# Moving five small tiles ahead of the stationary operands in SBUF

## The chip, the core and the metric

One core of a Trainium2 chip runs the whole kernel as one program. The metric is the device time of one execution in microseconds (us); of several executions the median is given. The engines are TensorE (PE in the profile, its weight loads PEld), VectorE (DVE), ScalarE (ACT), GpSimd (POOL) and SyncE (SP, which issues most transfers).

## The reference

One layer of a decoder trunk on x of 256 x 2048 in float32:

```python
h = h + 0.5 * swiglu_ffn(rms_norm(h, ffn1_norm), ffn1_w_gate, ffn1_w_up, ffn1_w_down)   # 2048 -> 5632 -> 2048
hn = rms_norm(h, mix_norm)
proj = hn @ w_in                                     # q | k | v | u, 1024 columns each
attn = mixture_of_dilations(rms_norm(q), rms_norm(k), v, rel_bias)   # 8 heads of 128
y = s5_ssm(u, lambda, log_dt, b, c, d)               # 64 groups of 16 channels, 64 complex states each
y = gelu(y); y = y * sigmoid(y @ glu_w + glu_b)
h = h + concat([attn, y]) @ w_out
h = h + 0.5 * swiglu_ffn(rms_norm(h, ffn2_norm), ffn2_w_gate, ffn2_w_up, ffn2_w_down)

def swiglu_ffn(x, w_gate, w_up, w_down):
    return (silu(x @ w_gate) * (x @ w_up)) @ w_down
```

## The kernel before, in words

The big products are all done by one loop, `run` (lines 247 to 330), over a list of passes: 22 gate and up passes and 4 down passes of the first feed-forward (`ffn`), the mixer's passes (`w_in`, `glu_w`, `w_out`), then 22 and 4 again. A pass makes 512 output columns for all 256 rows. Its weights come in groups of four blocks of 128 rows, 1 MB each, into `raw` (three buffers, SyncE's queue). Each group is handled as two units. For a unit, ScalarE writes the high part of the weights, rounded to the matmul's reduced format, to `wh` (line 281), and VectorE the rest, `raw - wh`, to `wl` (line 286); four buffers each let the splits run ahead of TensorE by up to four units. Then TensorE does twelve matmuls of 128 x 128 by 128 x 512: for each of two blocks and two halves of the rows, high by high (line 325), high by low (326) and low by high (327). The weights `wh`, `wl` are the moving operand, 512 columns at a time; the stationary operand is 128 x 128 of the transposed activations, also in a high and a low tile:

- in the gate and up passes and in `w_in`: `xth` and `xtl`, four pairs of tiles [128, 4, 256] in the pool `const` (class `Normed`, `open`, lines 156 and 157);
- in the down passes: `hid`, tiles [128, 2, 4, 256] (high and low together) in the pool `slots`;
- in `glu_w` and `w_out`: tiles in `slots` as well, which the profile calls by their tags `slot`, `s4b`, `s2a` and `s2b`.

A gate and up result is turned for the down product by `by_blocks` (line 124): VectorE transposes it in 32 x 32 blocks into `blocks`, a transfer writes that to memory (`h_d`), four transfers bring it back into `sil`, and ScalarE and VectorE split it into `hid` (lines 119, 120). The code of such side work is in generators, each advanced one step after every unit (`step`), so its instructions stand in each engine's queue between the splits, in a fixed order.

During the first feed-forward `ssm_prepare` computes the tables of the state-space model in this way, most of it VectorE's work (the powers in lines 654 to 656). In the mixer, `ssm_run` does the scan on VectorE (lines 767 to 769), and the attention's heads go on beside it.

SBUF is laid out when the program is built. The pools lie one behind the other, `const`, `slots`, `rawp`, `wp`, `sm`, `sm1`. Within a pool a tile takes its place when its tag is first asked for, right behind the tile before it, its size rounded up to 32 bytes of a partition. `slots` starts at the next place behind the last tile of `const`.

Of the kernel before, what the change touches and what calls it, by code (L numbers as in the profile page):

```python
# [9 lines left out]
F32 = mybir.dt.float32  # L10
# [6 lines left out]
P = 128  # L17
# [29 lines left out]
def hybrid_layer_kernel(  # L47
# [10 lines left out]
    const = ctx.enter_context(tc.tile_pool(name="const", bufs=1))  # L58
# [19 lines left out]
    def small(shape, tag):  # L78
        p = sm1 if tag in ("rel", "knc") else sm
        return p.tile(list(shape), F32, name=nm(tag), tag=tag)  # L80

    def tps():
        return tpp.tile([P, 512], F32, name=nm("tp"), tag="tp")
# [7 lines left out]
    rq = const.tile([P, 2, 8], F32, name="rq", tag="rq")  # L91
    stat = const.tile([P, NH, 8], F32, name="stat", tag="stat")
    a8 = const.tile([P, 2, 2, NG], F32, name="a8", tag="a8")

    m1_d = dram.tile([4, 4, P, 512], F32, name="m1_d", tag="m1_d")
    m2_d = dram.tile([4, P, 2048], F32, name="m2_d", tag="m2_d")
# [121 lines left out]
    def spawn(g, delay=0):  # L218
        gens.append([g, delay])
        return g  # L220
# [177 lines left out]
    def residual(norm, factor):  # L398
        def done(n):
            def f(acc):  # L400
                for t in range(NT):
                    vec.scalar_tensor_tensor(out=res[n][:, t, :], in0=acc[t], scalar=factor,
                                             in1=res[n][:, t, :], op0=ALU.mult, op1=ALU.add)
                spawn(norm.feed(n) if n == 3 else norm.feed_by_blocks(n))
            return f
        return done

    def final(n):
        def f(acc):
            for t in range(NT):  # L410
                vec.scalar_tensor_tensor(out=res[n][:, t, :], in0=acc[t], scalar=0.5,
                                         in1=res[n][:, t, :], op0=ALU.mult, op1=ALU.add)
                (sync if n == 3 else pool).dma_start(out=out[0, t * P:(t + 1) * P, n * 512:(n + 1) * 512], in_=res[n][:, t, :])
        return f


    def ssm_prepare():
# [3 lines left out]
        def T():  # L421
            i = tmpi[0]
            tmpi[0] += 1
            assert i < 36
            return a3[:64, i * 64:(i + 1) * 64]

        lr, li = T(), T()
        ldt = const.tile([64, 1], F32, name="ldt", tag="ldt")
        pool.dma_start(out=ldt, in_=ssm_log_dt[0].rearrange("(g o) -> g o", o=1))
        pool.dma_start(out=lr, in_=ssm_lambda_re[0])  # L430
        pool.dma_start(out=li, in_=ssm_lambda_im[0])
# [36 lines left out]
            vec.scalar_tensor_tensor(out=em, in0=p2, scalar=-1.0, in1=e, op0=ALU.add, op1=ALU.add)  # L468
            res_.extend((ex, em))

        col = const.tile([64, 8], F32, name="dtcol", tag="dtcol")
        ci = [0]

        def newcol():
# [153 lines left out]
        ps = tps()  # L628
        pe.transpose(ps[:, 0:16], dpad.rearrange("q j c -> q (j c)"), ident[:16, :16])
        yield  # L630
        dcol = const.tile([P, 16], F32, name="dcol", tag="dcol")
        act.activation(out=dcol, in_=ps[:, 0:16], func=AF.Copy)
        dmask = const.tile([P, 16], F32, name="dmask", tag="dmask")
        vec.tensor_tensor(out=dmask, in0=ident[:, 0:16], in1=ident[:, 32:48], op=ALU.add)
        vec.tensor_tensor(out=dmask, in0=dmask, in1=ident[:, 64:80], op=ALU.add)
        vec.tensor_tensor(out=dmask, in0=dmask, in1=ident[:, 96:112], op=ALU.add)
# [433 lines left out]
    with tc.manual_schedule():  # L1070
        xin = x[0].rearrange("(t p) d -> p t d", p=P)
        grow = slots.tile([50, P], F32, name="grow", tag="s5a")
        act.dma_start(out=grow[0:16], in_=ffn1_norm[0].rearrange("(k p) -> k p", p=P))
        sync.dma_start(out=res[0][:, :, 0:256], in_=xin[:, :, 0:256])
        warm = const.tile([1, 1], F32, name="warm", tag="warm")
        vec.memset(warm, 0.0)
        act.activation(out=warm, in_=warm, func=AF.Silu)
        make_identity(nc, ident)

        def warm_up(n):  # L1080
            ps = tps()
            for _ in range(n):
                pe.transpose(ps[:, 0:P], ident, ident)

        warm_up(12)
        ps = tps()
        pe.transpose(ps[:, 0:16], grow[0:16], ident[:16, :16])
        vec.tensor_copy(out=gains["f1"], in_=ps[:, 0:16])

        def other_gains():  # L1090
            for i, g in enumerate((mix_norm, ffn2_norm)):
                pool.dma_start(out=grow[16 + 16 * i:32 + 16 * i], in_=g[0].rearrange("(k p) -> k p", p=P))
            pool.dma_start(out=grow[48:49], in_=q_norm)
            pool.dma_start(out=grow[49:50], in_=k_norm)
            pool.memset(flip, 0.0)
            pool.affine_select(out=flip, in_=flip, compare_op=ALU.not_equal, fill=1.0, base=1 - P,
                               pattern=[[1, P]], channel_multiplier=1)
            pool.memset(sgn[0:64], 1.0)
            pool.memset(sgn[64:128], -1.0)
            yield 4  # L1100
            ps = tps()
            pe.transpose(ps[:, 0:50], grow, ident[:50, :50])
            for i, key in enumerate(("mx", "f2")):
                vec.tensor_copy(out=gains[key], in_=ps[:, 16 + 16 * i:32 + 16 * i])
            knc = small([P, 1], "knc")
            vec.tensor_copy(out=knc, in_=ps[:, 49:50])
            vec.scalar_tensor_tensor(out=qkg, in0=ps[:, 48:49], scalar=1.0 / math.sqrt(HD), in1=knc,
                                     op0=ALU.mult, op1=ALU.mult)
            yield
            yield from bias_table()  # L1110

        def bias_table():
            rel = small([34, NH], "rel")
            pool.memset(rel, 1.0)  # L1114
            pool.dma_start(out=rel[0:32], in_=rel_bias)
            oh = slots.tile([34, SPAN], F32, name="oh", tag="s1a")
            pool.dma_start(out=oh, in_=bias_rows)
            yield
            yield
            ps = tps()  # L1120
            pe.matmul(ps[:NH, 0:SPAN], rel, oh, start=True, stop=True)
            bt = slots.tile([NH, SPAN], F32, name="bt", tag="s1b")
            vec.tensor_copy(out=bt, in_=ps[:NH, 0:SPAN])
            pool.dma_start(out=b_d, in_=bt)

        n1, nmix, n2 = Normed("f1"), Normed("mx"), Normed("f2")

        feeds = [n1.feed(n, True) for n in range(4)]

        def feed_input():  # L1130
            for n in range(1, 4):
                for _ in feeds[n]:
                    pass
                yield 2 if n < 3 else 1
            spawn(other_gains())
            mx["pre"] = spawn(ssm_prepare(), 1)
            for n in range(4):
                n1.squares(n)
                n1.count()
                yield  # L1140

        def start():
            next(feeds[0], None)
            if "go" not in mx:
                warm_up(4)
            if "go" in mx:
                spawn(feed_input())
            mx["go"] = True

        ff1 = ffn(n1, ffn1_w_gate[0], ffn1_w_up[0], ffn1_w_down[0], residual(nmix, 0.5), True)  # L1150
        mixp = mixer(nmix, residual(n2, 1.0))
        ff2 = ffn(n2, ffn2_w_gate[0], ffn2_w_up[0], ffn2_w_down[0], lambda n: final(n), False)

        def load_x(n):
            if n == 0:
                sync.dma_start(out=res[0][:, :, 256:512], in_=xin[:, :, 256:512])
            elif n < 4:
                sync.dma_start(out=res[n], in_=xin[:, :, n * 512:(n + 1) * 512])

        run(ff1 + mixp + ff2, load_x, start)  # L1160
# [54 lines left out]
```

## Time and profile before

| | |
|---|---|
| median of 3 runs | 1856.63 us (1852.51 to 1858.55) |
| the profiled execution | 1858.62 us, its span 1856.8 us |
| mean granted TensorE clock | 0.993 |
| transferred | 401.23 MB, mean 216 GB/s |

How to read the rows. The span is the time from the first to the last profiled instruction. A group of instructions shows: line, engine, operation, tiles (out<-in), shapes and count, then the time in which at least one of them was under way, the mean duration of one in ns, and how long the engine was idle just before them and for whom. Matmuls overlap: each lasts longer than the distance from its start to the next one's. A row of stretches shows, for PE, PEld, DVE, ACT and POOL, the busy time and the instructions (x) in the stretch, then the granted clock (PEclk), the share of the transfer engines and GB/s; asked for one tile, it shows the instructions of that tile alone and only the engines that have any. A row of the timeline shows start, duration, engine, line, operation, tiles and, in brackets, the idle time before and who ended it. The chain of waits is followed back from the end, at each step to the work that released it; cut to a stretch, its first row gives shares of that stretch by engine and line.

### The profile page before, as it was taken

To read this page: it belongs to the slowest core of one execution; us is meant where nothing else is said; L and a number is where in the kernel's file an instruction comes from. 1 tells how busy PE (TensorE), PEld (TensorE's weight loads), DVE (VectorE), ACT (ScalarE), POOL (GpSimd) and SP (SyncE) were. 2 spreads that over 40 slices of the span, in tenths; PEclk is the share of its full clock that TensorE was granted. 3 is DMA by queue.
4 is the path that set the end of the run, shared out by engine and by line. 5 is a ranking of instruction groups with operands and counts; after the bars stand their busy time and mean duration, and the time that the engine had idled before them with its cause. 6 is when DMAs were issued, how large, how long until landed. Compare 5 with 4: busy or idle time off the path is not lost.

```text
span 1856.8 us, 21467 instructions
## 1 busy us (share of the span) xinstructions
PE 1825.0 (98%) x8389; PEld 1476.3 (80%) x8389; DVE 1061.3 (57%) x1382; ACT 836.1 (45%) x1071; POOL 42.8 (2%) x91
## 2 busy tenths in 40 slices
PE   8999999999999999989999999999999999999999
PEld 6787777788888888867877888888888888888887
DVE  4778788555554555534795665555555555544443
ACT  5444434344444444435566555444444444443332
POOL 2100000000000000010000001000000000000000
PEclk8999999999999999989999999999999999999999
DMA  8676788866766666598556586667666666666562
GB/s 268 204 207 191 252 268 274 258 204 211 216 218 212 208 225 207 194 256 282 181 190 223 202 243 206 205 208 216 214 204 209 218 207 205 218 211 212 197 214 103
DMA packets 220389, 401.23 MB, mean 216 GB/s; under 512 B 9580, under 2 KB 50133, under 8 KB 219136
## 3 DMA queue, kind: packets, MB, share of 16 engines
q1 hardware_dynamic: 214384, 383.29, 65.3%
q0 software_dynamic: 4080, 13.43, 2.3%
q10 hardware_dynamic: 1824, 3.15, 0.6%
q8 instruction: 65, 1.06, 0.2%
q14 instruction: 36, 0.29, 0.0%
HBM read 370.00 MB, written 32.45 MB: 217 GB/s over the span
## 4 chain that ended last, share of the span: by engine, by line
PE 82%; DVE 8%; DMA 6%; ACT 2%; issue 1%; SPq 1%; ACTq 0%; DVEq 0%
PE acc L325 26%; PE acc L326 26%; PE acc L327 26%; DVE wl L286 3%; DMA h_d<-blocks 2%; DMA sil<-h_d 1%; DMA raw<-in_ffn_w_gate_dram 1%; DVE s4b L654 1%; ACT wh L281 1%; DMA raw<-in_w_in_dram 1%; DVE s1a L767 1%; DMA u_d<-s4a 0%; DVE slot L655 0%; DVE s1a L768 0%; DVE s4a L656 0%
## 5 line engine op out<-in xcount | busy, mean ns | idle before, releaser
L286 DVE TENSOR_TENSOR wl<-raw,wh 128x1024 fp32r<-128x1024 f32 x628 | 765.6, 1225 | 669.6 <-ACT wh L281 669.3
L281 ACT ACTIVATE wh<-raw 128x1024 fp32r<-128x1024 f32 (+1 forms) x636 | 667.2, 1057 | 857.4 <-PE acc L327 796.5
L325 PE MATMUL acc<-wh,xth 128*128 128x512 f32 x1664 | 666.5, 401 | 16.9 <-ACT wh L281 16.9
L326 PE MATMUL acc<-wl,xth 128*128 128x512 f32 x1664 | 662.3, 398 | 3.7 <-DVE wl L286 3.5
L327 PE MATMUL acc<-wh,xtl 128*128 128x512 f32 x1664 | 660.4, 397 | 0.0
L325 PEld LDWEIGHTS acc<-wh,xth 128*128 128x128 f32 x1664 | 314.5, 189 | 95.1 <-ACT wh L281 19.5
L326 PEld LDWEIGHTS acc<-wl,xth 128*128 128x128 f32 x1664 | 314.4, 189 | 82.9 <-DVE wl L286 8.7
L327 PEld LDWEIGHTS acc<-wh,xtl 128*128 128x128 f32 x1664 | 314.4, 189 | 75.3
L326 PE MATMUL acc<-wl,hid 128*128 128x512 f32 x704 | 273.9, 389 | 0.0
L327 PE MATMUL acc<-wh,hid 128*128 128x512 f32 x704 | 273.9, 389 | 0.0
L325 PE MATMUL acc<-wh,hid 128*128 128x512 f32 x704 | 273.9, 389 | 0.0
L326 PEld LDWEIGHTS acc<-wl,hid 128*128 128x128 f32 x704 | 132.1, 188 | 27.6
L327 PEld LDWEIGHTS acc<-wh,hid 128*128 128x128 f32 x704 | 132.1, 188 | 27.5
L325 PEld LDWEIGHTS acc<-wh,hid 128*128 128x128 f32 x704 | 132.1, 188 | 27.4
L120 DVE TENSOR_TENSOR hid<-sil,hid 128x512 fp32r<-128x512 f32 x44 | 28.5, 689 | 67.9 <-ACT hid L119 67.9
L119 ACT ACTIVATE hid<-sil 128x512 fp32r<-128x512 f32 x44 | 25.4, 624 | 87.5 <-DMA sil<-h_d 87.5
L369 DVE SCALAR_TENSOR_TENSOR sil<-acc,rstd,sil 128x512 f32<-128x512 f32 x44 | 30.8, 741 | 0.0
L358 ACT ACTIVATE sil<-acc,rstd 128x512 f32<-128x512 f32 x44 | 27.5, 675 | 3.6 <-POOL rel L1114 3.6
L129 DVE STREAM_TRANSPOSE blocks<-sil 128x512 f32<-128x512 f32 x44 | 28.5, 685 | 0.0
L113 POOL TENSOR_TENSOR rs_t<-rstd 128x2 f32<-128x2 f32 x9 | 3.6, 396 | 665.9 <-DVE rstd L110 665.4
L325 PE MATMUL acc<-wh,slot 128*128 128x512 f32 x48 | 18.9, 393 | 0.0
L327 PE MATMUL acc<-wh,slot 128*128 128x512 f32 x48 | 18.7, 390 | 0.0
(324 smaller groups left out, 793.5 us busy)
## 6 DMA issues: line engine op xcount, KB each, us to landing
raw<-in_ffn_w_up_dram SPq DMA_DIRECT2D x88, 1024.0 KB, 5.8
raw<-in_ffn_w_down_dram SPq DMA_DIRECT2D x88, 1024.0 KB, 5.1
raw<-in_ffn_w_gate_dram SPq DMA_DIRECT2D x87, 1024.0 KB, 5.6
raw<-in_w_in_dram SPq DMA_DIRECT2D x32, 1024.0 KB, 5.6
raw<-in_w_out_dram SPq DMA_DIRECT2D x16, 1024.0 KB, 5.8
h_d<-blocks SPq DMA_DIRECT2D x28, 512.0 KB, 6.9
sil<-h_d SPq DMA_DIRECT2D x88, 128.0 KB, 6.9
m_d<-slot POOLq DMA_DIRECT2D x4, 1024.0 KB, 7.0
```

What stands on the lines that cost most here:

```text
L119: act.activation(out=h, in_=src, func=AF.Copy)
L120: vec.tensor_tensor(out=l, in0=src, in1=h.bitcast(F32), op=ALU.subtract)
L129: vec.transpose(out=b[:, :, t].rearrange("p j (k c) -> p j k c", k=4), in_=src[:, t, :].rearrange("p (k j c) -> p j k c", k=4, j=4))
L281: act.activation(out=h[:, c], in_=src[:, c], func=AF.Copy)
L286: vec.tensor_tensor(out=l, in0=src, in1=h.bitcast(F32), op=ALU.subtract)
L325: pe.matmul(acc[t], sh[:, c], h[:, kk, :], start=first, stop=False)
L326: pe.matmul(acc[t], sh[:, c], l[:, kk, :], start=False, stop=False)
L327: pe.matmul(acc[t], sl[:, c], h[:, kk, :], start=False, stop=last)
L358: act.activation(out=sil[c][:, t, :], in_=acc[t], func=AF.Silu, scale=norm.scale(t))
L369: vec.scalar_tensor_tensor(out=a[:, t, :], in0=acc[t], scalar=norm.scale(t), in1=a[:, t, :], op0=ALU.mult, op1=ALU.mult)
L654: vec.tensor_tensor(out=t_, in0=zb, in1=pr, op=ALU.mult)
L767: vec.tensor_tensor(out=tm, in0=a8, in1=prev.unsqueeze(1).broadcast_to([P, 2, 2, NG]), op=ALU.mult)
```

## The change

Five small tiles of the pool `const` are asked for at the start, behind `a8`, instead of where they are first used. Four belong to `ssm_prepare`: `ldt` and `col` (`dtcol`), which were asked for behind `xth` and `xtl`, and `dcol` and `dmask`, which were asked for behind `blocks`. The fifth, `warm`, was asked for at the start of the work and stays in its neighbourhood.

```diff
     a8 = const.tile([P, 2, 2, NG], F32, name="a8", tag="a8")
+    ldt = const.tile([64, 1], F32, name="ldt", tag="ldt")
+    col = const.tile([64, 8], F32, name="dtcol", tag="dtcol")
+    dcol = const.tile([P, 16], F32, name="dcol", tag="dcol")
+    dmask = const.tile([P, 16], F32, name="dmask", tag="dmask")
+    warm = const.tile([1, 1], F32, name="warm", tag="warm")
...
         lr, li = T(), T()
-        ldt = const.tile([64, 1], F32, name="ldt", tag="ldt")
...
-        col = const.tile([64, 8], F32, name="dtcol", tag="dtcol")
         ci = [0]
...
-        dcol = const.tile([P, 16], F32, name="dcol", tag="dcol")
         act.activation(out=dcol, in_=ps[:, 0:16], func=AF.Copy)
-        dmask = const.tile([P, 16], F32, name="dmask", tag="dmask")
...
-        warm = const.tile([1, 1], F32, name="warm", tag="warm")
         vec.memset(warm, 0.0)
```

The instructions of every engine, their order and their waits are the same in both programs; only the addresses of some tiles differ. In bytes of a partition:

| tiles | address before | modulo 512 | address after | modulo 512 |
|---|---|---|---|---|
| `ldt`, `dtcol` | 68512, 68544 | 416, 448 | 35520, 35552 | 192, 224 |
| `dcol`, `dmask` | 72672, 72736 | 480, 32 | 35584, 35648 | 256, 320 |
| `warm` | 35520 | 192 | 35712 | 384 |
| sums and factors of the norms (`ssp`, `rstd`) | 35552 to 35712 | | 35744 to 35904 | |
| `xth`, `xtl`, four pairs | 35744 + n x 4096 | 416 | 35936 + n x 4096 | 96 |
| `blocks` | 68576 | 480 | 68704 | 96 |
| all of `slots` (`hid` and others) | from 72800 | 96 | the same | 96 |
| `raw` | 171104 + n x 8192 | 96 | the same | 96 |
| `wh`, `wl` | 195680 + n x 4096 | 96 | the same | 96 |
| `ident`, `flip`, `res` | 16512 to 33920 | 128 | the same | 128 |

Within a tile, a matmul's operand starts at a multiple of 512 bytes, so the residue of the tile holds for all its operands.

## The prediction

> **What bounds the kernel now.** I read the page's busy times first, then the groups of instructions by line and form, then the busy time by stretches, then TensorE's timeline where one product follows another, and last the chain of waits stretch by stretch.
>
> ```profile
> PE 1825.0 (98%) x8389; PEld 1476.3 (80%) x8389; DVE 1061.3 (57%) x1382; ACT 836.1 (45%) x1071; POOL 42.8 (2%) x91
> L325 PE MATMUL acc<-wh,xth 128*128 128x512 f32 x1664 | 666.5, 401 | 16.9 <-ACT wh L281 16.9
> L327 PE MATMUL acc<-wh,xtl 128*128 128x512 f32 x1664 | 660.4, 397 | 0.0
> L325 PE MATMUL acc<-wh,hid 128*128 128x512 f32 x704 | 273.9, 389 | 0.0
> ```
>
> TensorE is busy 98% of the span. Three groups of 1664 matmuls (4992) take their stationary operand from `xth`/`xtl`, three of 704 (2112) from `hid`. The shape is the same, the moving operands are the same `wh`/`wl` tiles, yet one lasts 397 to 401 ns and the other 389. Matmuls overlap, so the cost is the distance between starts; a row of a long stretch with nothing but big matmuls gives it.
>
> ```profile
> core 0: us, PE busy (x) PEld busy (x) DVE busy (x) ACT busy (x) POOL busy (x), PEclk, DMA share, GB/s
> 540.00:770.00 230.00, 230.00 (x1016) 190.46 (x1015) 120.56 (x127) 99.81 (x111) 0.00 (x0) 1.00 0.65 211
> 1140.00:1600.00 460.00, 460.00 (x1973) 370.65 (x1972) 236.63 (x223) 196.88 (x208) 0.00 (x0) 1.00 0.68 210
> ```
>
> From 540 to 770 us (`hid`) 1016 matmuls, less two that hang over the edges, make 230/1014 = 226.8 ns each; from 1140 to 1600 us (`xth`) 460/1971 = 233.4 ns. TensorE is never idle in either, and the granted clock is 1.00 in both. The `xth` products pay 6.6 ns more per matmul, 4992 x 6.6 = 32.9 us in all. What differs is the address of the stationary tile: `hid` lies at 96 modulo 512 like `wh` and `wl`, `xth` and `xtl` at 416. The switch from one to the other, in TensorE's timeline:
>
> ```profile
> 536.81 0.39 PE L327 MATMUL acc<-wh,xtl 128*128 128x512 f32 x1
> 537.04 0.39 PE L325 MATMUL acc<-wh,hid 128*128 128x512 f32 x1
> ...
> 538.43 0.39 PE L325 MATMUL acc<-wh,hid 128*128 128x512 f32 x1
> 538.65 0.39 PE L326 MATMUL acc<-wl,hid 128*128 128x512 f32 x1
> ```
>
> The six `hid` starts up to 538.43 still lie 0.23 apart (1.39/6 = 232 ns), from there on 0.22 to 0.23 (226.8 as above). So the fast pace sets in some seven matmuls after a disturbance. The same happens where small transposes interrupt products whose stationary tile is also at 96:
>
> ```profile
> 1044.16 0.60 PE L837 MATMUL tp<-ident,s1a 128*128 128x128 f32 x4
> 1044.52 0.47 PE L325 MATMUL acc<-wh,s4b 128*128 128x512 f32 x1
> 1044.83 0.39 PE L326 MATMUL acc<-wl,s4b 128*128 128x512 f32 x1
> ...
> 1046.21 0.39 PE L326 MATMUL acc<-wl,s4b 128*128 128x512 f32 x1
> ```
>
> Between 1044.83 and 1046.21 stand six starts, 230 ns each: an interruption costs the fast pace for about seven matmuls.
>
> **The change part by part.** It removes and adds no instruction, no wait and no transfer, and the order on every engine stays; five small tiles (192 bytes) move ahead, so `xth` and `xtl` go from 416 to 96 modulo 512 and `blocks` from 480 to 96; `wh`, `wl`, `hid` and the rest stay. `ldt`, `col`, `dcol`, `dmask` and `warm` themselves cost the same at another place: no row shows a dependence of VectorE on it, and the changes are multiples of 32 bytes. `blocks` is written by VectorE and read by a transfer; `hid`'s neighbours at 96 do both already; I cost it at nothing.
>
> What remains is 6.6 ns for each of 4992 matmuls, wherever TensorE sets the end. That is what the chain of waits tells, cut into stretches.
>
> ```profile
> by line: DVE wl L286 20.4%; DMA h_d<-blocks 17.3%; DMA sil<-h_d 10.9%; issue 8.0%; DVE s4b L654 6.8%; DVE slot L655 3.9%; DVE s4a L656 3.5%; DVE s4a L655 3.1%; DMA k_d<-slot 3.0%; SPq L690 3.0%; DVE s4b L669 2.8%; DVE sil L369 2.6%; SPq L13
> by line: DVE wl L286 27.6%; DVE s1a L767 13.7%; DVE s1a L768 11.0%; issue 8.1%; DVE slot L769 8.1%; ACT wh L281 4.3%; ACT tp L844 4.0%; DVE rs_t L115 2.4%; DVE rs_t L113 2.3%; DVE rs_t L114 2.3%; DVE s5a L909 2.3%; DVE s5a L907 2.0%; DVE st
> by line: DMA raw<-in_w_in_dram 34.5%; DMA u_d<-s4a 27.8%; DMA slot<-m_d 20.6%; DVE wl L286 3.9%; PE acc L326 3.8%; ACT wh L281 3.3%; PE acc L327 2.7%; ACT s4a L976 2.2%; PE acc L325 1.3%; issue 0.8%; ACTq L281 0.1%; SPq L702 0.1%; SPq L268
> by line: PE acc L327 33.3%; PE acc L325 33.3%; PE acc L326 33.3%; PE tp L184 0.2%
> ```
>
> The first is 152 to 356 us (VectorE's powers of the state-space model, then the turn of a hidden block through `h_d`), the second 886 to 955 (the scan), the third 800 to 832 (loads behind `u_d`), the last 1084 to 1612 (gate and up of the second feed-forward). In the first three TensorE hardly stands in the chain: what it gains there it waits longer. In the last it is all. The other stretches are TensorE's too. How many matmuls of lines 325 and 326 with `xth` each holds (line 327's come to half as many again):
>
> ```profile
> 22.00:152.00 130.00, 110.00 (x343) 64.31 (x343) 3.31 (x8) 3.12 (x8) 0.98 0.69 213
> 152.00:356.00 204.00, 171.81 (x532) 100.11 (x530) 0.00 (x0) 0.00 (x0) 0.99 0.79 252
> 356.00:537.00 181.00, 162.58 (x518) 97.01 (x516) 0.00 (x0) 0.00 (x0) 1.00 0.71 218
> 776.00:800.00 24.00, 20.56 (x66) 12.22 (x66) 1.75 (x4) 1.68 (x4) 1.00 0.62 186
> 832.00:886.00 54.00, 40.93 (x124) 23.22 (x124) 0.00 (x0) 0.00 (x0) 0.97 0.88 281
> 886.00:955.00 69.00, 54.10 (x169) 30.91 (x168) 0.00 (x0) 0.00 (x0) 1.00 0.57 174
> 955.00:1003.00 48.00, 28.76 (x88) 15.95 (x88) 0.00 (x0) 0.00 (x0) 1.00 0.67 235
> 1084.00:1612.50 528.50, 442.21 (x1407) 264.38 (x1408) 8.19 (x28) 5.97 (x15) 1.00 0.69 211
> ```
>
> The terms, times 6.6 ns: 1084 to 1612, 1407 x 1.5 = 2111 matmuls, 13.9 us. 356 to 537, 777, 5.1. 776 to 800, 99, 0.6. In three stretches small work interrupts:
>
> ```profile
> 22.00:152.00 130.00, 130.00 (x571) 103.58 (x570) 90.14 (x179) 67.97 (x107) 5.87 (x18) 0.98 0.69 213
> 832.00:886.00 54.00, 54.00 (x355) 43.07 (x354) 24.18 (x35) 30.10 (x52) 0.00 (x0) 0.97 0.88 281
> 955.00:1003.00 48.00, 47.93 (x445) 39.51 (x446) 30.55 (x68) 28.52 (x56) 0.54 (x1) 1.00 0.67 235
> ```
>
> From 22 to 152 us 571 less 515 leaves 56 small ones; in groups of four to eight that is 7 to 14 interruptions, 50 to 100 matmuls at the old pace, so 2.7 of 3.4 us. From 832 to 886 (186 big ones, 169 small) I take 0.5 of 1.2, from 955 to 1003 (132 and 313) 0.3 of 0.9. The stretches 152 to 356, 800 to 832 and 886 to 955 stand at zero; were they TensorE's after all, they would give 798 x 6.6 = 5.3, 0.7 and 1.7. Sum: 13.9 + 5.1 + 0.6 + 2.7 + 0.5 + 0.3 = 23.1 us.
>
> One cost comes with it. In 152 to 356 us TensorE runs dry four times, and a longer pause can lower its clock:
>
> ```profile
> 197.58 0.40 PE L327 MATMUL acc<-wh,xtl 128*128 128x512 f32 x1
> 199.20 0.50 PE L325 MATMUL acc<-wh,xth 128*128 128x512 f32 x1 [1.23 <-ACT wh L281]
> ...
> 200.92 0.63 PE L327 MATMUL acc<-wh,xtl 128*128 128x512 f32 x1
> ...
> 203.91 0.47 PE L325 MATMUL acc<-wh,xth 128*128 128x512 f32 x1
> 353.91 0.50 PE L325 MATMUL acc<-wh,xth 128*128 128x512 f32 x1 [1.49 <-ACT wh L281]
> ```
>
> After the pause at 197.58 the matmuls up to 203.9 last 0.63 us instead of 0.40 and start 0.43 apart, some 8 x 0.2 = 1.6 us lost. After the one before 353.91 they did not. Each pause grows by what TensorE gains in its 50 us, some 1.3 us, so the last may now be followed by slow matmuls too, and there TensorE sets the end: 0 to 1.6 us, I take 1. The other three lose it inside a stretch that VectorE and the transfers pace.
>
> Covers. Behind TensorE, ScalarE's and VectorE's splits must stay ahead. The tightest place I found outside the three stretches is a turned block that ScalarE waits for in its queue, with the splits behind it:
>
> ```profile
> 1375.37 1.15 ACT L119 ACTIVATE hid<-sil 128x512 fp32r<-128x512 f32 x2 [4.52 <-DMA sil<-h_d]
> 1378.65 3.50 DVE L286 TENSOR_TENSOR wl<-raw,wh 128x1024 fp32r<-128x1024 f32 x3 [1.33 <-ACT wh L281]
> 1381.02 0.40 PE L326 MATMUL acc<-wl,xth 128*128 128x512 f32 x1
> ```
>
> Three `wl` take 3.50 us from 1378.65; the first is done at about 1379.9, and its matmul starts at 1381.02, 1.1 us later. Between the block's issue and this use TensorE does about six units of twelve matmuls, which at 6.6 ns come 0.5 us sooner: the cover holds by 0.6. If it did not, each such block would cost up to 1 us; of the 22 (eleven to each feed-forward) some 16 lie outside the first stretch.
>
> So 23.1 - 1 = 22.1 us off. The profiled execution took 1858.6 us (span 1856.8), so 1836.5; the median of the three runs shown is 2.0 below it, so 1834.5.
>
> **The rivals.** First, no change: the pace hangs on something else in which `xth` differs, for example that it lies in the lower part of the memory, and 192 bytes don't alter that. For it speaks that no row shows a second residue for the same tile; against it that `xtl` of the last block ends 4 KB below `hid`'s first tile, and that h and l, both row halves and all four blocks of `xth` keep the same pace. It gives 1856.6. The Trainium skill, "TensorE: Matmul & The Clock Gate", section "Step-by-step: what each phase is for", is on this side: it says that TensorE has two independent read ports for the moving operand and for the weights, so that loading the next weights takes no read bandwidth from the running matmul. By that rule where the stationary tile lies could not matter and the sum would be zero; the trace's two paces for one shape don't agree with it, though they don't say that the address is the reason.
>
> Second, the covers fail: the turned blocks come late for a TensorE that runs ahead, in both feed-forwards. At 1 us for each of 16 blocks the gain falls to 6 us: 1850.6. The 4.52 us wait above speaks for it, the 1.1 us margin against it.
>
> Third, slower: the clock. The faster pace would last from 1084 to the end, 770 us, while the longest fast stretch now is 244 (1612 to 1857). Were the clock lowered after some 240 us of it, 510 us would run at a lower clock; the 22.1 us are used up at a granted clock of 510/532 = 0.96, and at 0.90 the time is 1834.5 + 57 = 1891. Against it: 540 to 770 us shows 1.00 at the fast pace throughout.
>
> **How the numbers follow.** The pace goes over to the `xth` products: 0.82. No change: 0.08. Covers fail: 0.05. The clock, or another loss above the gain: 0.05. Within 0.3% (5.6 us) is about what a measurement of this kernel can't tell from no change. Faster: 0.82 plus half of the covers' case and a little, 0.85; same 0.10; slower 0.05. The range goes from the full 32.9 us (1823) to what the two steady stretches leave (19.0) less 1.6 for the clock and some 5 us of late blocks (1844); it leaves out no change.
>
> **What would show it.** Right: `xth` groups at 389 to 393 ns instead of 397 to 401; from some point in the second feed-forward a stretch of 460 us holding about 2030 matmuls instead of 1973; that feed-forward's gate and up 14 us shorter; the stretch of the powers about as long as before, with longer pauses. Wrong: starts still 233 ns apart, or 227 with new waits of TensorE for `wh` or `wl` after each `hid`, or a PEclk below 1.00 late in the span.

## The result and the profile after

The changed kernel takes 1833.46 us (median of 4 runs, 1833.28 to 1834.23) against 1856.84 us of the kernel before beside it: a ratio of 0.9875, 95% interval 0.9863 to 0.9888, 23.4 us less. Its profiled execution took 1833.54 us with a span of 1831.8 us, 25.0 less than the span before. Line numbers of the changed kernel are five higher where the large products stand (330 to 332 for 325 to 327).

First the rows of the page and of the busy time by stretches that answer to those in the prediction:

```profile
PE 1798.0 (98%) x8389; PEld 1476.9 (81%) x8389; DVE 1060.3 (58%) x1382; ACT 834.7 (46%) x1071; POOL 43.4 (2%) x91
L330 PE MATMUL acc<-wh,xth 128*128 128x512 f32 x1664 | 658.7, 396 | 16.5 <-ACT wh L286 16.5
L332 PE MATMUL acc<-wh,xtl 128*128 128x512 f32 x1664 | 652.0, 392 | 0.0
L330 PE MATMUL acc<-wh,hid 128*128 128x512 f32 x704 | 274.0, 389 | 0.0
```

```profile
540.00:765.00 225.00, 225.00 (x994) 186.35 (x993) 116.92 (x123) 97.73 (x109) 0.00 (x0) 1.00 0.64 213
1130.00:1580.00 450.00, 450.00 (x1987) 372.64 (x1986) 238.68 (x226) 197.23 (x208) 0.00 (x0) 1.00 0.70 215
```

The engines' instructions are as many as before and `hid` is untouched: 225/992 = 226.8 ns between starts. The `xth` products now run at the same pace, 450/1985 = 226.7 ns, where it was 233.4. The clock is granted in full in both stretches. The chain of waits, cut to the powers of the state-space model and to gate and up of the second feed-forward:

```profile
by line: DVE wl L291 18.5%; DMA h_d<-blocks 16.3%; DMA sil<-h_d 8.6%; issue 6.9%; DVE s4b L655 6.5%; PE acc L331 4.5%; PE acc L332 4.1%; PE acc L330 4.1%; DVE slot L656 3.7%; DVE s4a L657 3.4%; ACT wh L286 3.0%; DVE s4a L656 3.0%; SPq L140 
by line: PE acc L331 33.3%; PE acc L332 33.3%; PE acc L330 33.3%; PE tp L189 0.2%
```

In the first, VectorE and the transfers still lead; TensorE has 13% of it. The second is TensorE's from end to end, as before.

Where the time came from can be read off the starts of the same matmul in two traces, since the order of TensorE's instructions is the same. The table has the length of each stretch in the two profiled executions, and beside it the means over several kernels of the experiments below: six in which the `xth` products start 232 to 234 ns apart (the kernel before and off32, off96, off128, off160, off224), three in which they start 227 ns apart (the changed kernel, all256, off256). Times in the first column are those of the kernel before, in us.

| stretch | before | after | less | mean of six | mean of three | less | predicted |
|---|---|---|---|---|---|---|---|
| 0 to 22, start | 22.0 | 23.2 | -1.2 | 22.5 | 23.0 | -0.6 | 0 |
| 22 to 152 | 130.0 | 126.4 | 3.6 | 129.5 | 126.4 | 3.1 | 2.7 |
| 152 to 356, powers | 203.5 | 200.7 | 2.8 | 202.0 | 201.3 | 0.8 | 0 |
| 356 to 537 | 181.5 | 178.5 | 3.0 | 182.0 | 177.2 | 4.8 | 5.1 - 1 |
| 537 to 776, `hid` | 239.2 | 239.1 | 0.0 | 239.1 | 239.1 | 0.0 | 0 |
| 776 to 800 | 24.0 | 23.4 | 0.6 | 24.0 | 23.4 | 0.6 | 0.6 |
| 800 to 832 | 30.2 | 29.9 | 0.3 | 30.0 | 30.2 | -0.3 | 0 |
| 832 to 886 | 55.8 | 54.4 | 1.4 | 55.1 | 54.3 | 0.8 | 0.5 |
| 886 to 955, scan | 68.9 | 68.9 | 0.0 | 68.9 | 68.9 | 0.0 | 0 |
| 955 to 1003 | 47.9 | 47.5 | 0.5 | 48.2 | 48.0 | 0.2 | 0.3 |
| 1084 to 1612 | 528.6 | 514.6 | 14.0 | 528.6 | 514.6 | 14.0 | 13.9 |

The stretches left out (1003 to 1084, and from 1612 on) are the same within 0.1 us. The last column sums to 22.1, the means to 23.4, the pair to 25.0.

### The profile page after: what moved, and what is told of

The parts are those of the page before. It is cut to its first block, busy times and chain, and to the rows that moved or that the text cites. A ratio compares the mean times of both kernels' runs of the same rounds, so it can differ in the third digit from the quotient of the medians.

```text
span 1831.8 us, 21467 instructions
## 1 busy us (share of the span) xinstructions
PE 1798.0 (98%) x8389; PEld 1476.9 (81%) x8389; DVE 1060.3 (58%) x1382; ACT 834.7 (46%) x1071; POOL 43.4 (2%) x91
## 4 chain that ended last, share of the span: by engine, by line
PE 84%; DVE 8%; DMA 5%; ACT 1%; issue 1%; SPq 1%; ACTq 0%; DVEq 0%
PE acc L330 27%; PE acc L331 27%; PE acc L332 27%; DVE wl L291 3%; DMA h_d<-blocks 2%; DMA sil<-h_d 1%; DMA raw<-in_ffn_w_gate_dram 1%; DVE s4b L655 1%; ACT wh L286 1%; DMA raw<-in_w_in_dram 1%; DVE s1a L768 1%; DVE s1a L769 0%; DVE slot L656 0%; DVE s4a L657 0%; DVE s4a L656 0%
## 5 line engine op out<-in xcount | busy, mean ns | idle before, releaser
L330 PE MATMUL acc<-wh,xth 128*128 128x512 f32 x1664 | 658.7, 396 | 16.5 <-ACT wh L286 16.5
L331 PE MATMUL acc<-wl,xth 128*128 128x512 f32 x1664 | 653.9, 393 | 3.6 <-DVE wl L291 3.2
L332 PE MATMUL acc<-wh,xtl 128*128 128x512 f32 x1664 | 652.0, 392 | 0.0
L330 PE MATMUL acc<-wh,slot 128*128 128x512 f32 x48 | 18.9, 393 | 0.0
L331 PE MATMUL acc<-wl,slot 128*128 128x512 f32 x48 | 18.7, 389 | 0.0
```

Of the source, the lines that this page charges most:

```text
L330: pe.matmul(acc[t], sh[:, c], h[:, kk, :], start=first, stop=False)
L331: pe.matmul(acc[t], sh[:, c], l[:, kk, :], start=False, stop=False)
L332: pe.matmul(acc[t], sl[:, c], h[:, kk, :], start=False, stop=last)
```

## Experiments

Theory A: TensorE's pace in these products depends on where the stationary tile lies relative to the moving one, by their distance modulo some size. Rival B: it depends on the stationary tile's own residue, 96 being a good one. All kernels are variants of the changed kernel unless said otherwise, with unused bytes put ahead of one group of tiles. Each was run once, except the pair at the end of this section (four runs each); a pace is read inside one trace, over 220 or 430 us, and is good to 0.1 to 0.2 ns, since a matmul more or less changes it by that much.

**Everything moved together, and the moving tiles moved alone.** all256 puts 256 bytes ahead of `xth`, so that all operands go from 96 to 352 modulo 512; wp192 puts 192 bytes ahead of `wh` and `wl` in a pool of their own; the pools `sm` and `sm1` behind them move along, no tile of which takes part in these products.

```diff
+    const.tile([P, 64], F32, name="pad_all", tag="pad_all")      # all256, behind a8
...
+    padp = ctx.enter_context(tc.tile_pool(name="padp", bufs=1))  # wp192, between rawp and wp
+    padp.tile([P, 48], F32, name="pad_w", tag="pad_w")
```

> The changed kernel with 256 unused bytes ahead of xth in the pool const: every operand of the big products (xth, xtl, hid, wh, wl) moves from 96 to 352 modulo 512, all still equal. Theory A (what counts is where the stationary tile lies relative to the moving one): 226.8 ns between starts in xth and hid products, about 1833 us. Rival B (the residue of the stationary tile by itself, 96 good, others bad): 233.4 ns in both, about 1833 + 7100 x 0.0066 x 0.9 = 1875 us.

> The changed kernel with 192 unused bytes ahead of wh and wl alone: xth, xtl and hid stay at 96 modulo 512, the moving tiles go to 288, so that all stationary tiles lie 192 bytes behind (modulo 512), as xth did in the kernel before. Theory A: 233.4 ns between starts in xth and hid products alike; the kernel before's 1856.8 plus 2112 x 6.6 ns = 13.9 for hid and up to 3 for glu_w and w_out: 1871 to 1874 us. Rival B: nothing changes against the changed kernel, 226.8 ns and 1833 us.

Measured: all256 1833.29 us and wp192 1876.97 us, with 1857.6 for the kernel before beside them. Busy time by stretches, first all256 (`hid`, then `xth`), then wp192 (the same two):

```profile
540.00:760.00 220.00, 220.00 (x972) 182.22 (x971) 114.05 (x119) 95.75 (x107) 0.00 (x0) 1.00 0.65 212
1140.00:1570.00 430.00, 430.00 (x1899) 356.04 (x1898) 228.44 (x216) 185.49 (x195) 0.00 (x0) 1.00 0.70 217
```

```profile
540.00:760.00 220.00, 220.00 (x944) 177.27 (x943) 112.97 (x121) 93.72 (x105) 0.00 (x0) 1.00 0.63 208
1140.00:1570.00 430.00, 430.00 (x1846) 346.50 (x1845) 221.05 (x214) 184.04 (x195) 5.12 (x12) 1.00 0.66 208
```

With all operands at 352 the pace stays at 220/970 = 226.8 and 430/1897 = 226.7 ns. With the moving tiles alone moved, both kinds of product fall to 220/942 = 233.5 and 430/1844 = 233.2 ns, `hid` too, although no stationary tile has moved. Rival B falls; it is the distance that counts. wp192 is 3 to 6 us above the 1871 to 1874 expected. By the starts of the same matmuls its trace is 18.4 us longer than that of the kernel before: 14.0 in the two `hid` stretches and 1.8 in 1003 to 1084 (`glu_w` and `w_out`), as theory A asks, and 2.5 spread over the rest, 1.5 of it in 356 to 537, where this trace has 3.4 us at a lowered clock and that of the kernel before has none. What is left is that the expectation started from 1856.8 us, and the execution of the kernel before that was profiled took 1858.6.

**The size of the modulus, and other distances.** These put 32 to 256 bytes between `const` and `slots`. `xth` and `xtl` stay, while `slots` and the moving tiles go up together, so `xth` comes to lie that many bytes below the moving tiles, and `hid` stays level with them.

```diff
     a8 = const.tile([P, 2, 2, NG], F32, name="a8", tag="a8")
+    slots.tile([P, 64], F32, name="pad_slots", tag="pad_slots")  # off256; 16 columns in off64, and so on
```

> The changed kernel with 256 unused bytes between the pools const and slots: xth and xtl stay at 96 modulo 512, all of slots and the moving tiles go to 352, so xth lies 256 bytes off the moving tiles while hid stays equal to them. Theory A with a period of 512 bytes: xth at 233.4 ns, hid at 226.8, about 1857 us. Rival C (the period is 256 bytes or a divisor of it): xth at 226.8 ns, about 1833 us.

> The changed kernel with 64 unused bytes between the pools const and slots: xth lies 64 bytes off the moving tiles modulo 512, hid stays equal to them. Theory A, any difference costs the same: xth at 233.4 ns, about 1857 us. Rival D (nearness counts, or the period is 64 bytes): xth at 226.8 ns or between, 1833 to 1850 us.

> 128 unused bytes between const and slots: xth lies 128 bytes below the moving tiles modulo 256. So far, by distance (stationary less moving, modulo 256): 0 gives 226.7 ns between starts, 64 (the kernel before) 233.3, 192 gives 229.0 (that is 64 below). Theory A2 (a conflict by the distance modulo 256, the worst a quarter ahead): between 226.7 and 233.3 ns, 1833 to 1857 us. Rival E (banks of 128 bytes, or of a size that divides 128, so that 128 counts as 0): 226.7 ns, 1833 us.

> 32 unused bytes between const and slots: xth lies 32 bytes below the moving tiles. Theory A2 (graded by distance): 226.7 to 229 ns in xth, 1833 to 1841 us. Rival E (banks of 128 bytes or fewer, any difference inside a bank the same as the 64 below): 229 ns, 1841 us.

> 224 unused bytes between const and slots: xth lies 224 bytes below the moving tiles, that is 32 ahead modulo 256. Theory A2: between the 226.7 of distance 0 and the 233.3 of distance 64: about 230 ns, 1845 us. Rival F (the pace has its best not at equal addresses but a little ahead of them): below 226.7 ns, below 1833 us.

> 160 unused bytes between const and slots: xth lies 160 bytes below the moving tiles, 96 ahead modulo 256. Theory A2: beyond the 233.3 of 64 ahead it gets no better before 128: 230 to 234 ns, 1845 to 1860 us. Rival F (a better distance than equality exists on this side): below 226.7 ns, below 1833 us.

> 96 unused bytes between const and slots: xth lies 96 bytes below the moving tiles, the last distance of the eight at steps of 32 modulo 256. Measured so far between starts in xth: 0 below 226.7 ns, 32 below 233.3, 64 below 229.0, 128 below 232.4, 160 below 234.3, 192 below 233.4, 224 below 233.4. Theory A3 (only equal addresses modulo 256 give the full pace, 64 below is an exception): 232 to 234 ns, 1853 to 1859 us. Rival I (the 229.0 belongs to a valley that goes on to 96 below): 226 to 230 ns, 1832 to 1845 us.

The rows of the `xth` stretch, in fences by kernel, the kernel before first, then off256, off64, off128 and off160:

```profile
1140.00:1570.00 430.00, 430.00 (x1844) 346.47 (x1843) 220.87 (x208) 184.13 (x193) 0.00 (x0) 1.00 0.68 210
```

```profile
1140.00:1570.00 430.00, 430.00 (x1899) 355.98 (x1898) 228.71 (x217) 185.49 (x195) 0.00 (x0) 1.00 0.70 217
```

```profile
1140.00:1570.00 430.00, 430.00 (x1880) 352.84 (x1879) 226.60 (x215) 184.74 (x195) 0.00 (x0) 1.00 0.69 214
```

```profile
1140.00:1570.00 430.00, 430.00 (x1852) 348.63 (x1851) 221.48 (x208) 183.68 (x194) 0.00 (x0) 1.00 0.69 210
```

```profile
1140.00:1570.00 430.00, 430.00 (x1837) 345.67 (x1837) 221.23 (x208) 183.09 (x193) 0.00 (x0) 1.00 0.67 209
```

The only number to compare is the count of matmuls in the same 430 us (the figure in the first brackets, less two). All distances:

| kernel | `xth` less `wh`, modulo 256 | ns between starts | time, us | before beside it, us |
|---|---|---|---|---|
| changed kernel | 0 | 226.7 | 1833.46 | 1856.84 |
| off256 | 0 (256 below) | 226.7 | 1833.63 | 1857.6 |
| off224 | 32 | 233.4 | 1859.1 | 1856.88 |
| kernel before | 64 (192 below) | 233.4 | | |
| off160 | 96 | 234.3 | 1854.54 | 1856.88 |
| off128 | 128 | 232.4 | 1856.92 | 1856.88 |
| off96 | 160 | 233.4 | 1855.7 | 1858.28 |
| off64 | 192 | 229.0 | 1841.12 | 1857.6 |
| off32 | 224 | 233.3 | 1856.36 | 1856.88 |

Rival C holds: 256 bytes apart is as good as equal, so 512 is enough but not needed. off64 came as rival D forecast (between, 1841 us) and not as theory A did; but nearness falls with off32, and a period of 64 bytes with off128. Beyond that no smooth rule is left: A2 (graded by distance) forecast 226.7 to 229 ns for 32 bytes below and got 233.3, and about 230 for 32 ahead and got 233.4; E (banks of 128 bytes) forecast 226.7 for 128 and got 232.4; the search for a distance better than equality (F) and for a valley around 64 below (I) found none. What stands is A3: of the eight distances in steps of 32 bytes, equality is the only one at the full pace, 64 below is an exception at 229.0, and the other six lie between 232.4 and 234.3. Why 64 below is better than 32 or 96 below isn't known.

**One load of three out of line.** xtl_off lays out `const` in another order, with `xtl` at 416 and `xth` at 96 (the edit in short form):

```diff
-    ldt, col, dcol, dmask = ...                     # behind a8
...
         n1, nmix, n2 = Normed("f1"), Normed("mx"), Normed("f2")
+        for n in range(4):
+            const.tile([P, 4, SEQ], F32R, name=nm("xtl"), tag=f"xtl{n}")
+        ldt, col, dcol, dmask = ...                 # here, then the four xth
```

> The changed kernel with the pool const in another order: the four xtl first, at 416 modulo 512, then the small tiles, then the four xth, at 96. Of each three loads only xtl's lies off the moving tiles, by the 64 modulo 256 of the kernel before. Theory G (each matmul pays by itself, for the weights loaded beside it): a mean of 226.7 + 6.6/3 = 228.9 ns in xth and xtl products, about 1841 us, and one of the three starts late by 6 to 7 ns. Rival H (one load off the others upsets the rhythm of all): 233 ns, about 1857 us.

Measured: 1848.81 us, between the two forecasts. The rows of TensorE and of its weight loads in a piece of the timeline (lines 326 to 328 are here high by high, high by low and low by high):

```profile
1300.40 0.39 PE L326 MATMUL acc<-wh,xth 128*128 128x512 f32 x1
1300.40 0.19 PEld L327 LDWEIGHTS acc<-wl,xth 128*128 128x128 f32 x1
1300.63 0.39 PE L327 MATMUL acc<-wl,xth 128*128 128x512 f32 x1
1300.63 0.19 PEld L328 LDWEIGHTS acc<-wh,xtl 128*128 128x128 f32 x1
1300.86 0.40 PE L328 MATMUL acc<-wh,xtl 128*128 128x512 f32 x1
1300.86 0.19 PEld L326 LDWEIGHTS acc<-wh,xth 128*128 128x128 f32 x1
1301.09 0.39 PE L326 MATMUL acc<-wh,xth 128*128 128x512 f32 x1
```

Each weight load goes on beside the matmul before its own. Over the 1140 to 1570 us of that trace the distances after the starts of lines 326, 327 and 328 have means of 228.3, 229.2 and 235.8 ns: 231.1 on average, where one third of the penalty would be 228.9 and all of it 233.4. Neither forecast holds: one wrong load of three costs two thirds of the penalty. There is one slow interval of three, 9 ns longer, as theory G has it, while the others are 2 ns longer; and the slow one is not beside the load of `xtl` (under line 327) but the next. This unevenness can't be put down to the one load, though: in the traces of off96 and off64, where all three loads lie at the same distance, the same three means are 237.7, 230.8 and 231.5 ns, and 231.7, 225.8 and 229.2. Only the mean says something, that the cost is not simply one third for each load; which reads collide, and how, these runs don't tell. That reads of the stationary and the moving tile collide is a picture that fits them, not something a run showed.

**VectorE's powers made lighter.** The prediction put 152 to 356 us at zero, because VectorE and the transfers pace it. Both kernels were run with two of the three operations of each power left out:

```diff
-                vec.tensor_tensor(out=t_, in0=zb, in1=pr, op=ALU.mult)
-                vec.tensor_tensor(out=dst, in0=sb_, in1=pi, op=ALU.mult)
-                vec.tensor_tensor(out=dst, in0=dst, in1=t_, op=ALU.add)
+                vec.tensor_tensor(out=dst, in0=zb, in1=pr, op=ALU.mult)
```

> The kernel before with two of the three VectorE operations of each of the state-space powers left out (44 x 2 of about 0.65 us, 56 us of VectorE; the state-space part of the output is not the reference's). Both theories: the stretch of the powers (152 to 356 us) gets shorter and TensorE's pauses in it smaller, about 1845 us.

> The changed kernel with the same VectorE operations left out. Theory (in 152 to 356 us TensorE's gain is lost because VectorE's powers and the turn of a block pace that stretch): without them the stretch is TensorE's and the change is worth 3 to 5 us more than the 23.4 measured, 27 to 29 us between light_before and light_after. Rival (the gain there is lost to the restarts after each interruption, not to VectorE): 22 to 25 us between the two.

(There are 32 such triples, not 44, so some 42 us of VectorE went.) Measured: light_before 1845.49 us (1844.02 to 1847.42), light_after 1816.86 (1815.36 to 1818.40), against 1858.28 of the kernel before; ratios 0.9935 (0.9918 to 0.9953) and 0.9780 (0.9765 to 0.9796). The difference is 28.6 us, in the theory's 27 to 29 and above the rival's 25, though with these intervals it is uncertain by some 4 us. The traces say where it lies. The chain of waits from 152 to 330 us, light_before, then light_after:

```profile
by line: PE acc L325 33.0%; PE acc L327 32.5%; PE acc L326 32.4%; PE tp L676 2.3%
```

```profile
by line: PE acc L330 32.8%; PE acc L331 32.5%; PE acc L332 32.5%; PE tp L677 2.3%
```

The stretch is TensorE's now, in both, and its pauses are gone. By the starts of the same matmuls the change is worth 5.5 us there (all of the 5.3 that the prediction named as the upper bound), where the means of the full kernels have 0.8, and 4.8 us in 356 to 537. What the change could not give in that stretch was withheld by VectorE's powers.

## Why the prediction was right, step by step

It forecast 1834.5 us, 22.1 us less; measured were 1833.46 and 23.4. The mechanism was right; the agreement to 1.3 us is in part luck, since small terms that were off (the clock, the start, the powers, none above 1 us in the means) have different signs.

**The pace.** 6.6 ns for each `xth` matmul, read off `hid` beside `xth` in one trace: 233.4 to 226.7, as said. The reason given, equal residues, was an inference from one pair of residues; wp192 and all256 make it a shown one, and off256 shows 256 bytes to be the size that matters. The rival of no change falls with the result itself, and also with wp192: moving `wh` and `wl` by 192 bytes alone costs 43.5 us against the changed kernel (1876.97 less 1833.46). One of the signs named was missed: the mean of line 330 is 396 ns, not 389 to 393; a mean over the execution also has the interrupted and the slowed matmuls in it, and the distances in the long stretch are the measure. The Trainium skill, "TensorE: Matmul & The Clock Gate", section "Step-by-step: what each phase is for", says that loading weights takes no read bandwidth from the running matmul; by that one would expect the distance not to matter, the 226.7 and 233.4 ns measured differ from that, and they decide, though no run shows that read bandwidth is what is lost.

**The terms where TensorE sets the end.** 1084 to 1612 us: 13.9 forecast, 14.0 measured, in all three kernels at the new pace alike. 356 to 537: 5.1 less 1 for the clock, 3.0 in the pair and 4.8 in the means. The clock's cost did come in the pair, and it was all of the 1.6 us allowed; with 0.5 for late `wl` (under the covers, below) that leaves the 3.0. The changed kernel's timeline after the fourth pause:

```profile
347.03 0.39 PE L332 MATMUL acc<-wh,xtl 128*128 128x512 f32 x1
348.73 0.50 PE L330 MATMUL acc<-wh,xth 128*128 128x512 f32 x1 [1.32 <-ACT wh L286]
349.99 0.51 PE L331 MATMUL acc<-wl,xth 128*128 128x512 f32 x1 [0.76 <-DVE wl L291]
...
350.94 0.63 PE L331 MATMUL acc<-wl,xth 128*128 128x512 f32 x1
...
353.93 0.45 PE L332 MATMUL acc<-wh,xtl 128*128 128x512 f32 x1
```

From 350.9 to 353.9 matmuls last 0.63 us, as they did after the first pause before; the granted clock from 350.6 to 354.0 us is 0.50. But the step's reason, a longer pause, is wrong: this one (1.32 us idle) is shorter than the same one before (1.49, in the prediction), which left the clock alone. Nor does the cost come with the change: after the fourth pause the clock is lowered in two of the six kernels at the old pace (off32 and off128) and in one of the three at the new. Without this term the forecast was 23.1 us, nearer to what was measured.

**The stretches at zero.** The scan gave 0.0, the loads behind `u_d` nothing that stands out of the scatter. In the powers the pair shows 2.8 us, and that looked like a missed term; the means of six and three kernels have 0.8, and single kernels of the old pace reach from 199.4 to 204.6 us there. VectorE's part is fixed. From the first turned block's arrival (ScalarE, `hid`) to the next block's transposition (VectorE, `blocks`), first before, then after:

```profile
195.90 1.16 ACT L119 ACTIVATE hid<-sil 128x512 fp32r<-128x512 f32 x2 [8.66 <-DMA sil<-h_d]
227.71 1.26 DVE L129 STREAM_TRANSPOSE blocks<-sil 128x512 f32<-128x512 f32 x2
```

```profile
193.88 1.15 ACT L124 ACTIVATE hid<-sil 128x512 fp32r<-128x512 f32 x2 [9.95 <-DMA sil<-h_d]
225.70 1.26 DVE L134 STREAM_TRANSPOSE blocks<-sil 128x512 f32<-128x512 f32 x2
```

31.8 us in both, and in all twelve kernels of full work. What scatters is the way of the block through memory behind it, 22.4 to 26.0 us for the fourth in twelve traces, at the old pace and the new. The prediction's sentence that each pause would grow by 1.3 us held for the first alone: 1.6 us without a start became 3.2, the others went from 1.4, 1.5 and 1.9 to 1.0, 1.0 and 1.7, where those ways were shorter.

**The interrupted stretches.** 22 to 152: 2.7 taken of 3.4, 3.1 measured; 832 to 886: 0.5, 0.8 measured; 955 to 1003: 0.3, 0.2 measured. The differences from the forecast, 0.1 to 0.4 us, are no larger than those between kernels of one pace.

**The covers.** They held where the prediction looked. In 1073 to 1587 us of the changed kernel TensorE waits for nothing, though ScalarE's wait for turned blocks there, 31.3 us before, is longer:

```profile
ACT hid L124 <- DMA sil<-h_d: 40.7, 10, 4.6
```

In 351 to 529 us TensorE has no wait of its own, but two of its weight loads come late, for `wl`, which none did before in that stretch:

```profile
PEld acc L331 <- DVE wl L291: 0.8, 2, 0.4
```

At each, at 433.1 and 520.5 us, two matmuls start later than the pace, 0.5 us together. So in the first feed-forward the cover did fall short a little in this execution; the rival's 1 us for each block it was not.

**The clock as a slower rival.** The granted clock is 1.00 from 1048 us to the end of the work at 1831 and 0.992 over the span, against 0.993 before. Nothing of it came.

## What to carry to other kernels

Where the same matmul runs at two paces in one trace with the engine never idle, look for what differs in its operands' addresses: the fast group beside the slow one gives the price per instruction, and the chain of waits, stretch by stretch, tells where the price is paid (here 23 of 33 us). Here the stationary and the moving operand had to be equal modulo 256 bytes; a few small tiles in between are enough to lose that for a whole pool. And before a term of 2 or 3 us is explained from one pair of traces, compare the same stretch, and the clock in it, in several: here the 2.8 us of the powers lay within the scatter from kernel to kernel, and the clock's 1.6 us came and went at either pace.

## What the runs showed of the hardware that I had not expected

- The pace depends on the distance of the two operands modulo 256 bytes, but not smoothly: 226.7 ns at 0, 229.0 at 64 below, 232.4 to 234.3 at the six other steps of 32.
- One load of three out of line costs two thirds of the whole penalty (231.1 ns, between 226.7 and 233.4). The starts of three successive matmuls can be uneven even where all three loads lie at one distance (237.7, 230.8 and 231.5 ns in off96).
- A pause of 1.32 us before a matmul and 0.76 before the next was followed by 3.4 us at a granted clock of 0.50 in one execution, one of 1.49 and 0.75 in another was not. In all fourteen traces each lowered clock before the end of the work lasts 3.4, 6.8 or 10.2 us, that is one, two or three times the same length. The Trainium skill, "TensorE: Matmul & The Clock Gate", section "What's actually happening", says that the activity is judged in a free-running window; these lengths and the two pauses agree with that, though where a window begins is not to be seen in any run here. The table of that section has the clock fall after an idle window of about 3.4 us; before this fall TensorE was idle for 1.32 and 0.76 us only, so if a window without any work is meant, the measurement differs, and it decides.
